# Transposed blocks in two PSUM banks each, six blocks of w_down by row block, and the last norm on VectorE, in a two-layer hybrid decoder trunk

## The chip, the core and the metric

The kernel runs on one core of a Trainium2 chip. The metric is device time in microseconds (us) of one execution, lower is better; it is given as the median of several runs, and one execution was recorded by the hardware profiler. TensorE is called PE here as in the profile (PEld is its weight load), VectorE DVE, ScalarE ACT, GpSimd POOL; SyncE (SP) issues nearly all DMAs.

## The reference

Two layers over 512 tokens of width 1024, all in fp32. Each layer projects the modulated tokens, runs three token mixers (a gating MLP, retention, sparse attention), projects back, adds the residual and normalises. Then it runs a gated MLP of width 2816 with a causal convolution of width 3, adds and normalises again. What the change touches is the second half and the step from layer to layer:

```python
cond = jax.nn.silu(c)
for l in range(DEPTH):
    mod = cond @ w_ada[l] + b_ada[l]
    sh1, sc1, g1, sh2, sc2, g2 = [m[:, None, :] for m in jnp.split(mod, 6, axis=-1)]
    h = x * (1 + sc1) + sh1
    y = hybrid_mixer(h, w_in[l], ...)          # ends in @ w_out[l]
    x = layer_norm(DN_ALPHA * x + g1 * y, ln1_g[l], ln1_b[l])
    h = x * (1 + sc2) + sh2
    y = conv_ffn(h, w_up[l], conv_w[l], conv_b[l], w_down[l])   # (silu(gate) * up) @ w_down
    x = layer_norm(DN_ALPHA * x + g2 * y, ln2_g[l], ln2_b[l])
```

## The kernel before, in words

Tokens lie in four row blocks of 128 (t = 0 to 3), X[t] of 128x1024 each. Every fp32 operand of a large matmul is split into a rounded part (ACT casts it, "hi") and the rest (DVE subtracts, "lo"), and a product is three matmuls, hi hi, hi lo, lo hi (`mm3`, L448, whose matmuls are at L449 to L451).

Weights come by class `Weights` (L84). `jobs` lists them in order of use; `load` issues a DMA of 512 KB into one of three raw buffers, `split` (L125 on ACT, L127 on DVE) makes hi and lo in one of three buffer pairs or in a slot named in `slots`, and `next(key, ahead)` hands out one and splits up to `ahead` more. A raw buffer is free for the next DMA when both parts are made.

A compiler pass with a model of times lays the instructions in each engine's queue, which the engine then works through in order. What is wrapped in `pin` keeps the order of the program, what is `loose` may be placed elsewhere. Buffers come from pools by tag; an instruction that writes a new tile waits until the readers of the buffer's last tile are done. PSUM has eight banks of 128x512 fp32, all under tag "ps".

w_down is applied in 22 feature blocks of 128 (ct). The activations g of a block are split by `gsplit` (L1300) into tiles of tag "p" (five buffers). For ct 0 to 17 the loop at L1318 does a whole block: for each t and each half of 512 columns three matmuls, 24 in all, into eight banks pd[t][half]. The last four blocks (`LAST`, L380) are held, with their weights in slots of tag hB, and are done by row block at L1347: for t, for half, for the four blocks, so that row block 0 is complete first. What follows a row block differs by layer:

- In layer 0: `resid` (L1167: DVE multiplies the bank by the gate row, L1170, and adds to X, L1171), `bn_stats` (L1355), `stats` (L1175: DVE aggregates, POOL makes 1/std at L1178 and L1179), `normalize` (L1182, the instruction at L1183), and `finish`, which is `to_h` for the row block before. `to_h` (L427) transposes X[t] for the next layer: for each half q, four 128x128 transposes into one PSUM bank (L434), then DVE (L442) and ACT (L440) scale two blocks each, ACT casts all four (L444), DVE subtracts (at `sub`, L187). The queue order on DVE is: both halves of `resid` of t, `finish(t-1)` for q = 0, `normalize(t)`, `finish(t-1)` for q = 1. On PE the eight transposes of t-1 stand behind the matmuls of t. Row block 3's follow as `last_h` (L580) in the next layer, behind the first two half products of the key and value projections.
- In layer 1 (the end): POOL adds the residual for t < 3, t = 0 and 1 are normalised on DVE by two `scalar_tensor_tensor` (L1367, L1368), t = 2 on ACT (L1339) with rows on POOL and DVE (L1342), t = 3 on DVE in two halves (L1380, L1381); six DMAs write the output.

The gain and bias rows of layer 0's last norm are loaded at L1284 (`norm_rows`, L1153, two 512 KB DMAs and two ACT multiplications by ALPHA at L1160) and applied to X in layer 1 by `gains` (L1163, two DVE instructions of 128x1024 at L1164 and L1165): t = 0 and 1 behind the projection "za0" (L758), t = 2 and 3 in the retention mixer (L885), which runs beside the attention. `to_h` is also used in the middle of each layer (L1225, L1258), where its DVE work is loose.

Of the kernel before, what the change touches and what calls it, by code (L numbers as in the profile page):

```python
# [17 lines left out]
P = 128  # L18
# [130 lines left out]
def tile_trunk(ctx, tc, I, tab, out, layers=L):  # L149
# [230 lines left out]
    LAST = 4  # L380
    TC = 512
# [134 lines left out]
    for l in range(layers):  # L516
# [57 lines left out]
        if l:  # L574
# [8 lines left out]
            w1, w2 = compress_load(l)  # L583
            for j in range(6):
# [270 lines left out]
        def retention():  # L855
# [24 lines left out]
            for j, nm in enumerate(("rq", "rk")):  # L880
                def put(tp, pz, j=j):
# [3 lines left out]
                    if l and not tp:  # L885
                        last_gains(2 + j)
# [406 lines left out]
        for ct in range(NFF - LAST, NFF):  # L1293
            def slot():
                t = hB("wx").rearrange("p (h a) n -> p h (a n)", h=2)
                return t[:, 0, :], t[:, 1, :]
            ws.slots["dn", l, ct] = slot
        gtail = []

        def gsplit(ct):  # L1300
            if ct <= NFF - LAST:
                gh, gl = pt(F32R), pt(F32R)
            else:
                if not gtail:
                    gtail.extend(big("gt", F32R)[:, :1536].rearrange("p (a n) -> p a n", a=3) for _ in range(2))
                gh, gl = [g[:, ct - (NFF - LAST) - 1, :] for g in gtail]
# [6 lines left out]
        def down(t, half, ct, gp, wt, at=loose):  # L1313
            sl = slice(t * P, (t + 1) * P)
            wh, wl = [w[:, half * 512:(half + 1) * 512] for w in wt]
            mm3(pd[t][half], gp[0][:, sl], gp[1][:, sl], wh, wl, ct == 0, ct == NFF - 1, at)

        for ct in range(NFF - LAST):  # L1318
            wt = ws.next(("dn", l, ct))
            gs[ct + 1] = gsplit(ct + 1)  # L1320
            gp = gs.pop(ct)
            for t in range(NT):
                for half in range(2):
                    down(t, half, ct, gp, wt)
        wts = {}
        for ct in range(NFF - LAST, NFF):
            wts[ct] = ws.next(("dn", l, ct))
            if ct + 1 < NFF:
                gs[ct + 1] = gsplit(ct + 1)
# [4 lines left out]
        def norm_act(t, mv, c0, c1):  # L1334
# [84 lines left out]
```

## Time and profile before

| | us |
|---|---|
| median of 3 runs | 1406.48 (1403.56 to 1411.06) |
| the profiled execution | 1405.42 |
| its span in the profile | 1403.5 |
| PE busy | 1348.3 (96%) |
| DVE busy | 872.4 (62%) |
| ACT busy | 549.2 (39%) |
| POOL busy | 209.6 (15%) |

The span is the stretch between the first and last instruction of the profiled execution; the execution's own time is 1.9 us longer. In the profile, a row of the timeline gives an instruction's start and length in us, engine, line, operation, output<-inputs with shapes, and in brackets the engine's idle time before it and what ended it ("x2" merges two neighbours). A window row gives each engine's busy time in a stretch with the number of instructions, the clock granted to TensorE as a share of full speed (2.4 GHz), the busy share of the DMA engines and GB/s.

### The profile page before, as it was taken

To read this page: it belongs to the slowest core of one execution; us is meant where nothing else is said; L and a number is where in the kernel's file an instruction comes from. 1 tells how busy PE (TensorE), PEld (TensorE's weight loads), DVE (VectorE), ACT (ScalarE), POOL (GpSimd) and SP (SyncE) were. 2 spreads that over 40 slices of the span, in tenths; PEclk is the share of its full clock that TensorE was granted. 3 is DMA by queue.
4 is the path that set the end of the run, shared out by engine and by line. 5 is a ranking of instruction groups with operands and counts; after the bars stand their busy time and mean duration, and the time that the engine had idled before them with its cause. 6 is when DMAs were issued, how large, how long until landed. Compare 5 with 4: busy or idle time off the path is not lost.

```text
span 1403.5 us, 19590 instructions
## 1 busy us (share of the span) xinstructions
PE 1348.3 (96%) x7723; PEld 1108.5 (79%) x7723; DVE 872.4 (62%) x1422; ACT 549.2 (39%) x999; POOL 209.6 (15%) x206
## 2 busy tenths in 40 slices
PE   5999999899999999999989999999999999999995
PEld 4898675679978788778878987876998888888884
DVE  6767533847797787743477578475675555763337
ACT  3525334543533343332323354465253334333320
POOL 0311220325011120000000024112400000000005
PEclk9999999999999999999999999999999999999998
DMA  9832545413586674322532231111223334332221
GB/s 299 231 89 71 177 145 180 127 61 102 168 285 213 215 260 137 121 94 91 159 68 66 61 96 46 46 46 39 82 76 97 100 90 134 92 124 102 90 75 60
DMA packets 181896, 168.91 MB, mean 120 GB/s; under 512 B 23540, under 2 KB 161644, under 8 KB 181804
## 3 DMA queue, kind: packets, MB, share of 16 engines
q1 hardware_dynamic: 174252, 141.18, 33.0%
q0 software_dynamic: 7552, 26.48, 5.5%
q8 instruction: 61, 1.00, 0.3%
q14 instruction: 31, 0.25, 0.1%
HBM read 163.44 MB, written 2.10 MB: 118 GB/s over the span
## 4 chain that ended last, share of the span: by engine, by line
PE 83%; DVE 8%; ACT 3%; DMA 3%; POOL 1%; issue 1%; SPq 1%; DVEq 0%; ACTq 0%
PE ps L449 19%; PE ps L451 19%; PE ps L450 19%; PE ps L542 4%; PE ps L543 4%; PE ps L544 4%; PE ps L1028 3%; PE ps L327 2%; PE ps L1020 2%; PE ps L969 1%; PE ps L970 1%; DVE t L1170 1%; POOL xa L1171 1%; DVE pt L989 1%; DMA wraw<-in_w_up_dram 1%
## 5 line engine op out<-in xcount | busy, mean ns | idle before, releaser
L125 ACT CAST whi<-wraw 128x1024 fp32r<-128x1024 f32 (+3 forms) x187 | 185.6, 997 | 400.1 <-PE ps L450 229.5
L127 DVE TENSOR_TENSOR wlo<-wraw,whi 128x1024 fp32r<-128x1024 f32 (+3 forms) x161 | 186.4, 1162 | 168.7 <-ACT whi L125 168.3
L451 PE MATMUL ps<-h2h,wlo 128*128 128x512 f32 (+1 forms) x736 | 278.2, 378 | 0.0
L450 PE MATMUL ps<-h2l,whi 128*128 128x512 f32 (+1 forms) x736 | 277.2, 377 | 0.0
L449 PE MATMUL ps<-h2h,whi 128*128 128x512 f32 (+1 forms) x736 | 276.9, 377 | 0.0
L450 PEld LDWEIGHTS ps<-h2l,whi 128*128 128x128 f32 x736 | 138.2, 188 | 28.7 <-issue 1.7
L449 PEld LDWEIGHTS ps<-h2h,whi 128*128 128x128 f32 x736 | 138.1, 188 | 28.4 <-ACT whi L125 2.5
L451 PEld LDWEIGHTS ps<-h2h,wlo 128*128 128x128 f32 x736 | 138.3, 188 | 26.1 <-issue 0.8
L542 PE MATMUL ps<-whi,hh 128*128 128x256 f32 (+1 forms) x448 | 131.9, 294 | 0.0
L543 PE MATMUL ps<-wlo,hh 128*128 128x256 f32 (+1 forms) x448 | 128.9, 288 | 0.0
L544 PE MATMUL ps<-whi,hl 128*128 128x256 f32 (+1 forms) x448 | 127.3, 284 | 0.0
L450 PE MATMUL ps<-wlo,pt 128*128 128x512 f32 x288 | 113.9, 396 | 0.0
L449 PE MATMUL ps<-whi,pt 128*128 128x512 f32 x288 | 113.9, 396 | 0.0
L451 PE MATMUL ps<-whi,pt 128*128 128x512 f32 x288 | 111.8, 396 | 0.0
L542 PEld LDWEIGHTS ps<-whi,hh 128*128 128x128 f32 x448 | 85.4, 191 | 13.9 <-issue 11.3
L543 PEld LDWEIGHTS ps<-wlo,hh 128*128 128x128 f32 x448 | 85.5, 191 | 5.5 <-issue 5.2
L127 POOL TENSOR_TENSOR wlo<-wraw,whi 128x1024 fp32r<-128x1024 f32 x26 | 64.1, 2467 | 157.1 <-ACT whi L125 142.1
L544 PEld LDWEIGHTS ps<-whi,hl 128*128 128x128 f32 x448 | 85.4, 191 | 0.2 <-issue 0.2
L1171 POOL TENSOR_TENSOR xa<-xa,t 128x256 f32<-128x256 f32 (+1 forms) x24 | 26.8, 1121 | 368.0 <-DVE t L1170 368.0
L187 DVE TENSOR_TENSOR pt<-g,pt 128x512 fp32r<-128x512 f32 x32 | 22.1, 691 | 81.5 <-PE ps L450 79.9
L985 ACT ACTIVATE pt<-ps,sm 128x256 f32<-128x256 f32 (+2 forms) x96 | 55.7, 590 | 39.3 <-DVE sm L982 27.1
L1021 ACT COPY pT<-ps 128x128 f32<-128x128 f32 (+3 forms) x128 | 50.3, 436 | 46.8 <-PE ps L1020 46.2
(279 smaller groups left out, 2610.6 us busy)
## 6 DMA issues: line engine op xcount, KB each, us to landing
wraw<-in_w_up_dram SPq DMA_DIRECT2D x88, 512.0 KB, 3.8
araw<-in_w_ada_dram POOLq DMA_DIRECT2D x48, 512.0 KB, 5.1
wraw<-in_w_down_dram SPq DMA_DIRECT2D x44, 512.0 KB, 3.4
wraw<-in_w_ada_dram SPq DMA_DIRECT2D x32, 512.0 KB, 4.5
wraw<-in_w_in_dram SPq DMA_DIRECT2D x30, 512.0 KB, 3.9
wraw<-in_w_out_dram SPq DMA_DIRECT2D x16, 512.0 KB, 4.6
a<-in_w_ada_dram SPq DMA_DIRECT2D x14, 512.0 KB, 7.4
wraw<-in_w_in_dram SPq DMA_DIRECT2D x8, 384.0 KB, 8.3
```

The source lines that it names most:

```text
L125: self.nc.scalar.copy(f(hi), src)
L127: eng.tensor_tensor(f(lo), src, f(hi).bitcast(F32), op=OP.subtract)
L449: at(T.matmul(o, lh, rh, start=first, stop=False))
L450: T.matmul(o, lh, rl, start=False, stop=False)
L451: T.matmul(o, ll, rh, start=False, stop=last)
L542: T.matmul(o, a, wh[:, k - k0, :], start=(first and k == 0), stop=False)
L543: T.matmul(o, a, wl[:, k - k0, :], start=False, stop=False)
L544: T.matmul(o, b, wh[:, k - k0, :], start=False, stop=(last and k == KD - 1))
L985: A.activation(pp[e][:, :n], o[e], AF.Exp, bias=sm[:, 0, e:e + 1], accum_out=sm[:, 1, e:e + 1])
L1021: A.copy(PT[e][:, i:i + 3 * i + 1:3, :], pb[:, :(i + 1) * P].rearrange("p (j q) -> p j q", q=P))
L1028: T.matmul(po[64 * e:64 * e + 64, j * P:], VS[:, b, j, 64 * g:64 * g + 64], PT[e][:, 4 * j:4 * j + NT - j, :].rearrange("p a q -> p (a q)" ...
L1171: i = eng.tensor_tensor(X[t][:, c0:c0 + n], X[t][:, c0:c0 + n], tmp, op=OP.add)
```

## The change

1. `to_h` puts the four transposes of a half into two banks, two each. DVE reads its two blocks from the first bank, ACT its two from the second.
2. Six blocks (`TAIL`) instead of four are held for the row-block loop, in both layers. The two more are weights in slots of tag m4 in layer 0 and hA in layer 1; their g tiles are split six blocks ahead, in the main loop from ct = 10 on, and `ws.next` splits up to six weights ahead from ct = 13 on.
3. In layer 1 the norm is done on DVE alone: `piece` (multiply, add, `bn_stats`) and `norm_out` (two `scalar_tensor_tensor` steps, the second in pieces with a DMA each). Row block 3's second half is done in two pieces of 256 columns with PSUM banks of their own (`ends`); what the main loop summed for it is added to X early, behind row block 0.
4. The rows of layer 0's last norm are loaded and scaled in layer 1 (`last_rows`, behind `compress_load`), and `gains` stands in front of "za0" for t = 0, 1 and behind it for t = 2, 3.

```diff
-    LAST = 4
-    TC = 512
+    TAIL = 6
...
         for q in range(2):
-            pb = ps()
-            for j in range(4):
-                c = 4 * q + j
-                pin(T.transpose(pb[:, j * P:(j + 1) * P], src[:, c * P:(c + 1) * P], ident))
+            pb = [ps(), ps()]
+            for e in range(2):
+                for j in range(2):
+                    c = 4 * q + 2 * j + e
+                    pin(T.transpose(pb[e][:, j * P:(j + 1) * P], src[:, c * P:(c + 1) * P], ident))
...
-                o, i = h32[:, j * P:(j + 1) * P], pb[:, j * P:(j + 1) * P]
+                o, i = h32[:, j * P:(j + 1) * P], pb[j % 2][:, j // 2 * P:(j // 2 + 1) * P]
...
             w1, w2 = compress_load(l)
+            lrows = last_rows()
...
+        if l:
+            for t in range(2):
+                last_gains(t, *lrows)
         run(tm_all(("za0", l), gelu_into(U)))
         if l:
-            for t in range(2):
-                last_gains(t)
+            for t in range(2, 4):
+                last_gains(t, *lrows)
...
-                    if l and not tp:
-                        last_gains(2 + j)
...
-        lgr, lbr = norm_rows(l, "ln2_g", "ln2_b", ALPHA if l + 1 < layers else 1.0)
...
+        else:
+            lgr, lbr = norm_rows(l, "ln2_g", "ln2_b", 1.0)
...
+        nmain = NFF - TAIL
+        for ct in range(nmain, NFF):
+            def slot(own=hA if ct < NFF - 4 else hB):
...
+            ws.slots["dn", l, ct] = slot if last or ct >= NFF - 4 else pair_slots("m4", "m4")
...
-        for ct in range(NFF - LAST):
-            wt = ws.next(("dn", l, ct))
-            gs[ct + 1] = gsplit(ct + 1)
+        for ct in range(nmain):
+            wt = ws.next(("dn", l, ct), ahead=max(2, 2 * (ct - nmain) + 8))
+            if ct + 1 < nmain:
+                gs[ct + 1] = gsplit(ct + 1)
+            if ct >= nmain - TAIL:
+                gs[ct + TAIL] = gsplit(ct + TAIL)
...
+        def piece(t, j, c0, c1, o):
+            c = slice(c0, c1)
+            tmp = t2()[:, :c1 - c0]
+            pin(V.tensor_tensor(tmp, o[:, :c1 - c0], gr[:, c], op=OP.mult))
+            pin(V.tensor_tensor(X[t][:, c], X[t][:, c], tmp, op=OP.add))
+            if j is not None:
+                pin(V.bn_stats(bst[t][:, j, :], X[t][:, c]))
+        def norm_out(t, mv):
+            pin(V.scalar_tensor_tensor(X[t], X[t], mv[:, 0:1], lgr, op0=OP.subtract, op1=OP.mult))
+            for c0, c1 in ((0, 512), (512, D)) if t < NT - 1 else ((0, 512), (512, 768), (768, D)):
+                c = slice(c0, c1)
+                pin(V.scalar_tensor_tensor(X[t][:, c], X[t][:, c], mv[:, 3:4], lbr[:, c], op0=OP.mult, op1=OP.add))
+                nc.sync.dma_start(out[0, t * P:(t + 1) * P, c], X[t][:, c])
         for t in range(NT):
-            for half in range(2):
-                for ct in range(NFF - LAST, NFF):
-                    down(t, half, ct, gs[ct], wts[ct], loose if ct > NFF - LAST else pin)
...
+            cuts = (0, 512, 768, D) if last and t == NT - 1 else (0, 512, D)
+            for j, (c0, c1) in enumerate(zip(cuts, cuts[1:])):
+                for ct in range(nmain, NFF):
+                    down(t, c0, c1, ct, gs[ct], wts[ct], loose if ct > nmain else pin)
+                piece(t, j, c0, c1, ends.get(c0, pd[t][c0 // 512]))
+            mv = stats(t, bst[t], len(cuts) - 1, pin)
+            if last:
+                norm_out(t, mv)
+                if not t:
+                    piece(NT - 1, None, 512, D, pd[NT - 1][1])
                 continue
...
+            fin = finish(t - 1) if t else iter(())
+            next(fin, None)
+            normalize(t, mv, pin)
+            run(fin)
```

## Rows read from the trace of the kernel before

**Rows 1.** The page, part 1: busy time of each engine, share, instructions.

```profile
PE 1348.3 (96%) x7723; PEld 1108.5 (79%) x7723; DVE 872.4 (62%) x1422; ACT 549.2 (39%) x999; POOL 209.6 (15%) x206
```

**Rows 2.** Windows: length, PE, PEld, DVE, ACT, POOL busy, clock, DMA, GB/s.

```profile
727.20:743.10 15.90, 8.33 (x57) 8.16 (x58) 10.59 (x21) 4.60 (x9) 2.23 (x5) 0.89 0.00 0
743.10:760.00 16.90, 16.90 (x143) 16.90 (x144) 11.58 (x27) 8.06 (x14) 0.12 (x1) 1.00 0.14 40
...
775.70:782.00 6.30, 6.30 (x55) 6.30 (x55) 0.10 (x2) 1.64 (x2) 0.00 (x0) 1.00 0.23 67
...
1355.00:1388.00 33.00, 33.00 (x142) 26.28 (x141) 16.26 (x20) 1.57 (x2) 13.04 (x10) 1.00 0.05 19
1388.00:1403.50 15.50, 0.01 (x1) 0.00 (x0) 10.70 (x15) 1.24 (x1) 5.80 (x9) 0.57 0.25 96
```

**Rows 3.** Waits of PE from 713 to 745: us, times, longest.

```profile
PE ps L434 <- DVE xa L1183: 8.0, 3, 4.7
```

**Rows 4.** Timeline of DVE, end of layer 0.

```profile
712.22 0.68 DVE L1170 TENSOR_TENSOR t<-ps,grow 128x512 f32<-128x512 f32 x1
...
716.55 0.36 DVE L442 TENSOR_SCALAR t<-ps,ab 128x128 f32<-128x128 f32 x1
717.44 0.41 DVE L442 TENSOR_SCALAR t<-ps,ab 128x128 f32<-128x128 f32 x1 [0.53 <-ACT t L440]
719.02 0.69 DVE L187 TENSOR_TENSOR hl<-t,hh 128x512 fp32r<-128x512 f32 x1 [1.18 <-ACT hh L444]
719.63 0.81 DVE L1183 TENSOR_SCALAR xa<-xa,mv 128x1024 f32<-128x1024 f32 x1
...
723.49 0.68 DVE L1170 TENSOR_TENSOR t<-ps,grow 128x512 f32<-128x512 f32 x1
```

**Rows 5.** Timeline of ACT, step to layer 1.

```profile
744.27 0.81 ACT L440 ACTIVATE t<-ps,ab 128x128 f32<-128x128 f32 x2 [0.48 <-DVE t L442]
744.97 0.61 ACT L444 CAST hh<-t 128x512 fp32r<-128x512 f32 x1
```

**Rows 6.** Timeline of DVE, end of layer 1.

```profile
1374.96 2.29 DVE L1367 SCALAR_TENSOR_TENSOR xa<-xa,mv,lg 128x1024 f32<-128x1024 f32 x1
...
1378.37 1.27 DVE L1368 SCALAR_TENSOR_TENSOR xa<-xa,mv,lb 128x1024 f32<-128x1024 f32 x1
...
1397.57 1.40 DVE L1381 SCALAR_TENSOR_TENSOR xa<-xa,mv,lb 128x512 f32<-128x512 f32 x2
```

**Rows 7.** Timeline of POOL: end of layer 0, attention, end of layer 1.

```profile
716.73 0.22 POOL L1178 TENSOR_SCALAR mv<-mv 128x1 f32<-128x1 f32 x1 [5.27 <-DVE mv L1177]
...
844.54 5.97 POOL L127 TENSOR_TENSOR wlo<-wraw,whi 128x1024 fp32r<-128x1024 f32 x2 [0.56 <-ACT whi L125]
...
1376.14 1.20 POOL L1178 TENSOR_SCALAR mv<-mv 128x1 f32<-128x1 f32 x1
1377.41 0.57 POOL L1179 TENSOR_TENSOR mv<-mv,mhalf 128x1 f32<-128x1 f32 x1
```

**Rows 8.** Timeline of SP: the output's DMAs.

```profile
1379.66 19.66 SPq L1345 DMA_DIRECT2D out_dram<-xa  x6
```

**Rows 9.** Waits of PE from 836 to 852, start of layer 1's attention.

```profile
PE ps L1020 <- DVE pt L989: 3.1, 3, 1.9
```

**Rows 10.** Timeline of DVE in the same stretch.

```profile
842.29 1.22 DVE L1164 TENSOR_TENSOR xa<-xa,lg 128x1024 f32<-128x1024 f32 x1
...
845.71 5.08 DVE L989 TENSOR_SCALAR pt<-pt,sm,gates 128x512 f32<-128x512 f32 x2
```

**Rows 11.** Timeline of ACT: w_down's weights, first and last of four casts.

```profile
1349.54 1.05 ACT L125 CAST wx<-wraw 128x1024 fp32r<-128x1024 f32 x1 [3.43 <-DMA wraw<-in_w_down_dram]
...
1355.29 1.05 ACT L125 CAST wx<-wraw 128x1024 fp32r<-128x1024 f32 x1 [2.28 <-DMA wraw<-in_w_down_dram]
```

**Rows 12.** The chain of waits in order of time, layer 1's second w_down block.

```profile
1279.14 1.40 PE ps L451 x6
```

**Rows 13.** Waits of PE from 330 to 360, middle of layer 0.

```profile
PE ps L434 <- DVE xa L1183: 1.4, 1, 1.4
```

More of the change, by code (lines that the diff above doesn't have):

```diff
@@ L1292, in tile_trunk @@
         bst = [pool.tile([P, 4, 6], F32, tag="bst", name="bst", bufs=4) for _ in range(NT)]
-        for ct in range(NFF - LAST, NFF):
-            def slot():
-                t = hB("wx").rearrange("p (h a) n -> p h (a n)", h=2)
+        last = l + 1 == layers
+        nmain = NFF - TAIL
+        for ct in range(nmain, NFF):
+            def slot(own=hA if ct < NFF - 4 else hB):
+                t = own("wx", F32R).rearrange("p (h a) n -> p h (a n)", h=2)
                 return t[:, 0, :], t[:, 1, :]
-            ws.slots["dn", l, ct] = slot
+            ws.slots["dn", l, ct] = slot if last or ct >= NFF - 4 else pair_slots("m4", "m4")
         gtail = []
         def gsplit(ct):
-            if ct <= NFF - LAST:
+            if ct <= nmain:
                 gh, gl = pt(F32R), pt(F32R)
+            elif ct > NFF - 3:
+                gh, gl = [pool.tile([P, 512], F32R, tag=("pcT", "yc")[NFF - 1 - ct], name="gt", bufs=2) for _ in range(2)]
             else:
@@ L1311, in tile_trunk, with down @@
         gs = {0: gsplit(0)}
-        def down(t, half, ct, gp, wt, at=loose):
+        def down(t, c0, c1, ct, gp, wt, at=loose):
             sl = slice(t * P, (t + 1) * P)
-            wh, wl = [w[:, half * 512:(half + 1) * 512] for w in wt]
-            mm3(pd[t][half], gp[0][:, sl], gp[1][:, sl], wh, wl, ct == 0, ct == NFF - 1, at)
-        for ct in range(NFF - LAST):
-            wt = ws.next(("dn", l, ct))
-            gs[ct + 1] = gsplit(ct + 1)
+            wh, wl = [w[:, c0:c1] for w in wt]
+            split = last and t == NT - 1 and c0 >= 512
+            if split and ct == nmain:
+                ends[c0] = ps()
+            o = (ends[c0] if split and ct >= nmain else pd[t][c0 // 512])[:, :c1 - c0]
+            mm3(o, gp[0][:, sl], gp[1][:, sl], wh, wl, ct == 0 or (split and ct == nmain),
+                ct == NFF - 1 or (split and ct == nmain - 1), at)
+        ends = {}
+        for ct in range(nmain):
[4 more added lines that the diff above has]
+                gs[ct + TAIL] = gsplit(ct + TAIL)
             gp = gs.pop(ct)
@@ L1323, in tile_trunk @@
                 for half in range(2):
[L1324 to L1329, printed above, removed]
+                    down(t, half * 512, half * 512 + 512, ct, gp, wt)
+        wts = {ct: ws.next(("dn", l, ct)) for ct in range(nmain, NFF)}
         def finish(t):
             return to_h(t, X[t], ab, *nxt_h, dve=pin)
-        def norm_act(t, mv, c0, c1):
-            nb = pool.tile([P, 2], F32, tag="nb", name="nb", bufs=2)
-            G.tensor_tensor(nb[:, 0:1], mv[:, 0:1], mv[:, 3:4], op=OP.mult)
-            G.tensor_scalar(nb[:, 1:2], nb[:, 0:1], -1.0, None, op0=OP.mult)
-            A.activation(X[t][:, c0:c1], X[t][:, c0:c1], AF.Identity, bias=nb[:, 1:2], scale=mv[:, 3:4])
@@ L1387, in last_h, with last_rows @@
                 return done(NT - 1)
-            def last_gains(t, gains=gains, lgr=lgr, lbr=lbr):
-                gains(t, lgr, lbr)
+            def last_rows(l=l, norm_rows=norm_rows):
+                return norm_rows(l, "ln2_g", "ln2_b", ALPHA)
+            last_gains = gains
 _INS = ['x', 'c', 'w_ada', 'b_ada', 'w_in', 'a_ln_g', 'a_ln_b', 'a_ws', 'a_bs', 'b_gn_g', 'b_gn_b',
```

37 lines of the change are left out of this document (1 added, 36 removed).

## The prediction

> **What bounds the kernel now.** I read the page first: PE is busy 96% of the span [rows 1], so time can only come from stretches where it waits. Then the windows around the two places that the change names [rows 2]. The reader is to see that PE is full (33.00 of 33.00 us) up to 1388.0, and then has nothing for 15.5 us: this is the end of the kernel. From 727.2 to 743.1, at the step from layer 0 to layer 1, it works 8.33 of 15.9 us; the waits of PE name DVE's `normalize` (L1183) for 8.0 us in three waits, the longest 4.7 [rows 3]. Last the timelines of DVE in these stretches, for what DVE is late with.
>
> Matmul costs come from full stretches: 33.0 us / 142 = 0.232 us for one of 512 columns, 16.9 / 143 = 0.118 us for one of 256 or a transpose [rows 2]. A row block of four held blocks is then 24 x 0.232 = 5.6 us of PE, one of six 36 x 0.232 = 8.4 us.
>
> **Step to layer 1 (parts 1 and 2).** One round of DVE runs from 712.22 to 723.49 [rows 4]: 11.27 us for a row block, against 5.6 + 0.9 (eight transposes) on PE. So DVE sets the pace. It consists of `resid`, `bn_stats` and aggregate (712.22 to 716.55, 4.3 us), a half of `to_h` (716.55 to 719.63, 3.1), `normalize` (0.7 to the next start) and the other half (3.1). Within a half, DVE and ACT take turns: DVE waits 0.53 for ACT between its two blocks and 1.18 for the cast [rows 4]. With a bank each, DVE's two blocks (0.72) run beside ACT's two; ACT's pair takes 0.70 to the cast's start and the cast 0.61 [rows 5], then the subtraction 0.69: about 2.05 us. The round becomes 4.3 + 2.05 + 0.7 + 2.05 = 9.1 us, and PE's becomes 8.4 + 0.9 = 9.3. Followed through from the first held block at time 0, `normalize` of row blocks 0 to 3 ends at 12.4, 21.8, 31.2 and 40.4, and PE comes to their transposes at 16.8, 26.1, 35.4 and 42.0 (the last behind 48 half-size products, 5.7 us). Nothing waits, the slack at the end is 1.6 us.
>
> What is there to win: the stretch of 15.9 us holds 48 + 8 instructions of 0.118, 6.6 us, so 9.3 are lost (the granted clock is 0.89 of 2.4 GHz there, so partly at the lower level of 1.2, after PE sat idle), and 0.4 before it, 9.7 in all. Against it stand four banks per `to_h` instead of two while all eight are in use: row block 0's second half must wait until DVE has multiplied row block 1's last bank, 0.7 us, less the transposes in front. I take 0.5, so **9.2 us gained**; if half of the waits stay it is 5, at best 9.7.
>
> Why DVE and ACT take turns the rows do not say: both also write one tile. The Trainium skill ("PSUM — Partial Sum Buffer", PSUM bank collisions raise a hardware error) says that two engines must not access one bank and quadrant at once, reads included, and may work on different banks. By that rule the turns end; without it the round stays at 11.3 (first rival).
>
> **Preparing six blocks.** Two more weights per layer must be split by the first held row block, whose first half takes 36/2 x 0.232 = 4.2 us. The order allows it from ct = 13 on, some 17 us ahead. The trace shows four casts within 6.8 us when buffers are free (from 1349.54 to the end of the one at 1355.29 [rows 11]), so six take 10 us and fit. The two held g tiles of ct = 16 sit in the five "p" buffers, so the lo part of the next block is made only when the block before is done: 0.7 us in five blocks of each layer, 7 us at most. But PE's order can put hi products first: six lo products ran in a row at 1279.14 [rows 12]. I take **0.5 us lost**, between 0 and 7.
>
> **End of layer 1 (part 3).** Now DVE's last instruction ends at 1399.0 (1397.57 + 1.40) [rows 6], 11.0 after PE, and the span ends 4.5 later, with the last of six DMAs issued by 1399.3 [rows 8]. After the change, per row block: two times 2.05 for `piece`, 0.15 for the aggregate, the first 1024-wide step, a wait for 1/std, and 1.4 for the second step. The first step takes 1.27 alone and 2.29 beside POOL's addition [rows 6]; that addition goes, so 1.25. The wait: POOL's L1178 took 0.22 beside PSUM-reading DVE work and 1.20 beside the step that started at 1374.96, ending with it; L1179 adds 0.57 and a gap [rows 7]. So DVE waits 0.8 behind its own step. Sum 7.7 us against 8.4 on PE, plus 1.35 once for the early piece of row block 3. Followed through, DVE reaches row block 3 at 30.8 (its first half is ready at 29.3), PE ends at 33.6, and DVE adds the last 256 columns by 35.1, then 0.15 + 1.25 + 0.8 + 0.7 + 0.4 + 0.4: end 38.7, 5.1 after PE instead of 11.0. That is 5.9 less 0.1 for 36 products of 256 in place of 18 of 512: **5.8 us gained**. The output takes nine DMAs instead of six; three lie behind DVE's last steps and the last one is small, so I leave 4.5. Bounds: 3 (DVE late by another half row block) and 7.0 (L1178 takes its 0.22 beside the step, so that the wait of 0.8 falls away in each row block and DVE is on time for row block 3).
>
> The Trainium skill ("SBUF — State Buffer", Who interferes with whom) speaks against this part: DVE with two SBUF inputs and a reading POOL instruction lock each other out for a whole instruction. The 1.20 beside 0.22 agrees with it; by that rule the gain is 5.8, without it the upper bound, 7.0.
>
> **Rows and gains (part 4).** Two DMAs and two ACT multiplications move from layer 0's up projection into layer 1's start, where SP and ACT have room; I cost them at nothing: behind these DMAs on SP stand the mixer's weights, and PE has the key, value and query projections to do before it needs those; without that cover PE would wait for a DMA as ACT does in [rows 11], some 3 us. They wait for m4 buffers that the two extra weights hold to the end of layer 0, as does the split of the second query weight (DVE 1.2 us, inside the 1.6 of slack above). The eight `gains` instructions of about 1.2 us [rows 10] move forward. DVE is nearly idle from 775.7 to 782.0 (0.10 busy) [rows 2], so they cost nothing there; if that cover is missing they cost up to 9.8. What they leave is the start of attention: PE waits 3.1 us for L989 [rows 9], and DVE runs a gain at 842.29 and then two L989 of 2.5 us each instead of one of them soon done, while POOL subtracts from 844.54 on [rows 7, 10]. Without the gains they start about 2 us earlier, before POOL. **2.0 us gained**, between 0 and 3.1.
>
> **Middle of the layers.** `to_h` there is loose and interleaved already; 1.4 us of waiting is the largest piece [rows 13]. Four banks per row block could as well cost a wait. **0.5 gained**, between -1 and 1.4.
>
> **Sum.** 9.2 - 0.5 + 5.8 + 2.0 + 0.5 = 17.0 us. The profiled execution took 1405.42, 1.1 below the median of 1406.48. 1405.4 - 17.0 = **1388.4 us**.
>
> **The rivals.** (1) The turns stay, because the shared output tile orders them: the round is 11.3, `normalize` of row block 3 ends at 45.2 instead of 40.4, PE comes at 42.0 and waits 3.2 us: 1391.6. For it: both engines write h32; against: different columns. (2) DVE falls behind at the end, and the 15.5 us stay: 1394. For it: 7.7 of 8.4 is little room; against: today's stretch is slowed by POOL additions that go. (3) The gains meet work that PE waits for: 9.8 us less 6.2 of idle time is 3.6, and the attention's wait stays: 1394. (4) Slower: the held weights are not ready. If only two of six are, and four come at the main loop's beat of 5.6 us, PE loses 4 x 5.6 - 4 x 0.7 = 19.6 us in each layer: 1428. It decides from 12 us per layer on. For it: casts wait for DMAs there, 3.43 and 2.28 [rows 11], and only three raw buffers exist; against: the pace of 1.7 us per cast in those rows.
>
> **How the numbers follow.** Forecast 0.60, rival 1 0.08, rival 2 0.10, rival 3 0.12, rival 4 0.05, and 0.05 for a mixture that gives back most. About 0.5%, 7.0 us, is what a measurement here can tell: faster means below 1398.4. Faster 0.60 + 0.08 + 0.09 + 0.08 = 0.85, same 0.10, slower 0.05. The range goes from the best bounds (9.7 + 7.0 + 3.1 + 1.4 = 21.2, rounded out to 1383) to the low ones together (5 + 3 + 0 - 1 - 3 for the g tiles = 4, 1401).
>
> **What would show it.** Right: L442 pairs without a wait for ACT, a DVE round near 9.1 us, no PE wait above 1 us at the step to layer 1; PE's end some 9 to 10 us before the span's; L1178 ending with DVE's first step of the norm; the 3.1 us at the attention mostly gone. Wrong: ACT casts of w_down ending after the first held matmul, PE waiting for a PSUM bank at the transposes, DVE's work in the last stretch more than 2 us behind PE, or new waits of PE near the first projection of layer 1.

## The result, and the profile after

The changed kernel took **1387.54 us** (median of 6 runs, 1385.30 to 1388.91), the kernel before beside it 1406.35 (6 runs, 1403.56 to 1411.06): a ratio of 0.9858, 95% interval 0.9845 to 0.9872. The profiled execution took 1387.29 with a span of 1385.5, so the spans differ by 18.0 us; the forecast was 17.0 and 1388.4.

Part 1 of the page of the changed kernel answers to [rows 1]: PE has lost 4 us of busy time and 14 us of waiting.

```profile
PE 1344.4 (97%) x7741; PEld 1107.8 (80%) x7741; DVE 871.7 (63%) x1436; ACT 545.0 (39%) x998; POOL 193.6 (14%) x196
```

The windows of the changed kernel, columns as in [rows 2]: the last 15.9 us before row block 3's transposes (the step), the last full stretch of PE, what comes after it, and the gains.

```profile
719.10:735.00 15.90, 15.90 (x102) 14.22 (x101) 13.16 (x24) 5.82 (x12) 2.32 (x5) 1.00 0.51 101
1341.50:1374.50 33.00, 33.00 (x160) 27.17 (x158) 24.31 (x36) 0.00 (x0) 5.64 (x6) 1.00 0.13 48
1374.50:1385.50 11.00, 0.00 (x0) 0.00 (x0) 5.18 (x11) 0.00 (x0) 1.88 (x2) 0.67 0.13 48
767.50:781.00 13.50, 13.50 (x146) 13.19 (x145) 11.71 (x11) 3.67 (x7) 0.00 (x0) 1.00 0.22 56
```

At the step PE now works 15.90 of 15.90 us where it worked 8.33 [rows 2], and in the list of its waits from 705 to 745 nothing is left of the 8.0 [rows 3]. During the gains PE is full too. After the last matmul 11.0 us remain instead of 15.5.

To see where the 18.0 us went, I cut each span at the starts of the same instructions: the first matmul of layer 0's projection by w_out (A ends), the last of its up projection (B), the first transpose of row block 3 at the step (C), the first matmul on tile F in layer 1's compression (D), the first of layer 1's projection by w_out (E), the last of its up projection (F), the last matmul (G), the end (H). Lengths in us, worked out from those starts:

```
kernel                    A       B       C      D       E       F       G      H    span
before                 278.42  320.89  143.72  40.61  169.07  311.81  123.10  15.90  1403.5
changed                279.63  321.23  134.10  40.54  164.20  311.19  123.33  11.29  1385.5
difference              +1.21   +0.34   -9.62  -0.07   -4.87   -0.62   +0.23  -4.61   -18.0
banks alone            275.40  320.87  138.78  40.61  169.02  311.36  123.10  15.91  1395.1
one bank               278.48  323.77  140.05  43.34  164.21  311.69  123.33  11.31  1396.2
four held blocks       276.25  321.26  138.60  40.61  164.17  311.12  123.24  19.79  1395.0
gains late             281.27  321.23  134.11  40.54  167.50  311.29  123.33  11.31  1390.6
std on ScalarE         277.59  321.27  134.08  40.54  164.25  310.87  123.33   8.01  1380.0
  once more            276.97  320.75  134.27  40.54  164.28  311.61  123.33   8.02  1379.8
  without the split    281.69  321.13  134.11  40.54  164.26  311.17  123.19   8.90  1385.0
  with late GpSimd work 280.73  321.39  134.24  40.54  164.28  311.35  123.33   9.77  1385.6
no split               280.97  320.72  134.30  40.54  164.21  311.18  123.19  11.30  1386.4
row in PSUM            279.73  321.47  134.10  40.55  164.18  311.15  123.33   9.54  1384.0
changed, once more     277.13  320.86  134.13  40.54  164.23  311.38  123.33  11.32  1382.9
```

The three indented rows are also of the kernel with std on ScalarE. Stretch A varies from profile to profile by 6 us, whatever the kernel; C, E and H repeat to 0.3 us or better where nothing in them was edited. So parts are compared by stretch, and the medians only confirm the sum. The change touches C (9.6), E (4.9) and H (4.6); these make 19.1, and A gave back 1.2 by chance.

The round of DVE at the step, timeline of the changed kernel, answers to [rows 4].

```profile
711.96 0.68 DVE L444 TENSOR_SCALAR t<-ps,ab 128x128 f32<-128x128 f32 x2
713.39 0.69 DVE L187 TENSOR_TENSOR hl<-t,hh 128x512 fp32r<-128x512 f32 x1 [0.74 <-ACT hh L446]
714.00 0.81 DVE L1187 TENSOR_SCALAR xa<-xa,mv 128x1024 f32<-128x1024 f32 x1
714.72 0.72 DVE L444 TENSOR_SCALAR t<-ps,ab 128x128 f32<-128x128 f32 x2
716.19 0.69 DVE L187 TENSOR_TENSOR hl<-t,hh 128x512 fp32r<-128x512 f32 x1 [0.74 <-ACT hh L446]
```

DVE's two blocks run without ACT between them ("x2", no wait), and a half takes from 711.96 to 714.00, 2.04 us, where it took 3.08 in [rows 4]. What is left is the wait of 0.74 for ACT's cast.

The end of layer 1, timeline of DVE in the changed kernel, first row block 1, then the last steps. It answers to [rows 6].

```profile
1360.90 1.28 DVE L1363 SCALAR_TENSOR_TENSOR xa<-xa,mv,lg 128x1024 f32<-128x1024 f32 x1
1362.95 1.42 DVE L1366 SCALAR_TENSOR_TENSOR xa<-xa,mv,lb 128x512 f32<-128x512 f32 x2 [0.77 <-POOL mv L1183]
...
1372.13 0.68 DVE L1356 TENSOR_TENSOR t<-ps,grow 128x512 f32<-128x512 f32 x1
...
1375.43 0.41 DVE L1356 TENSOR_TENSOR t<-ps,grow 128x256 f32<-128x256 f32 x1
...
1376.79 0.24 DVE L1181 BATCH_NORM_AGGREGATE mv<-bst 128x2 f32<-128x18 f32 x1
1377.07 1.28 DVE L1363 SCALAR_TENSOR_TENSOR xa<-xa,mv,lg 128x1024 f32<-128x1024 f32 x1
1379.12 1.54 DVE L1366 SCALAR_TENSOR_TENSOR xa<-xa,mv,lb 128x512 f32<-128x512 f32 x3 [0.77 <-POOL mv L1183]
```

From 1349.3 on DVE has no idle time but a wait of 0.77 for POOL in each of the four row blocks. It comes to the last 256 columns at 1375.43, 0.9 us after PE had done them, and ends at 1380.66. So DVE is what is late at the end now, not PE; what ties the end of the span to it is shown under "Why the closing is shorter". What DVE waits for is on POOL, in the same stretch (answers to [rows 7]).

```profile
1377.12 1.31 POOL L1182 TENSOR_SCALAR mv<-mv 128x1 f32<-128x1 f32 x1 [6.35 <-DVE mv L1181]
1378.51 0.57 POOL L1183 TENSOR_TENSOR mv<-mv,mhalf 128x1 f32<-128x1 f32 x1
```

### The profile page after: what moved, and what is told of

The parts are those of the page before. It is cut to its first block, busy times and chain, and to the rows that moved or that the text cites. A ratio compares the mean times of both kernels' runs of the same rounds, so it can differ in the third digit from the quotient of the medians.

```text
span 1385.5 us, 19644 instructions
## 1 busy us (share of the span) xinstructions
PE 1344.4 (97%) x7741; PEld 1107.8 (80%) x7741; DVE 871.7 (63%) x1436; ACT 545.0 (39%) x998; POOL 193.6 (14%) x196
## 4 chain that ended last, share of the span: by engine, by line
PE 85%; DVE 6%; DMA 3%; ACT 2%; POOL 1%; SPq 1%; issue 1%; POOLq 0%; DVEq 0%; ACTq 0%
PE ps L451 19%; PE ps L453 19%; PE ps L452 19%; PE ps L544 4%; PE ps L545 4%; PE ps L546 4%; PE ps L1032 3%; PE ps L327 2%; PE ps L1024 2%; DMA a<-in_w_ada_dram 1%; PE ps L973 1%; PE ps L974 1%; DMA wraw<-in_w_up_dram 1%; DMA wraw<-in_w_in_dram 1%; PE ps L1039 1%
## 5 line engine op out<-in xcount | busy, mean ns | idle before, releaser
L125 ACT CAST whi<-wraw 128x1024 fp32r<-128x1024 f32 (+4 forms) x183 | 181.5, 996 | 391.1 <-PE ps L452 235.5
L127 DVE TENSOR_TENSOR wlo<-wraw,whi 128x1024 fp32r<-128x1024 f32 (+3 forms) x157 | 181.6, 1162 | 160.9 <-ACT whi L125 157.6
L452 PE MATMUL ps<-wlo,pt 128*128 128x512 f32 x256 | 101.4, 396 | 0.0
L451 PE MATMUL ps<-whi,pt 128*128 128x512 f32 x256 | 101.2, 396 | 0.0
L544 PEld LDWEIGHTS ps<-whi,hh 128*128 128x128 f32 x448 | 85.4, 191 | 13.9 <-issue 11.3
L453 PE MATMUL ps<-whi,pt 128*128 128x512 f32 x256 | 90.4, 396 | 0.0
L1182 POOL TENSOR_SCALAR mv<-mv 128x1 f32<-128x1 f32 x16 | 9.0, 560 | 543.0 <-DVE mv L1181 543.0
L1279 ACT ACTIVATE t<-ps,pcol 128x512 f32<-128x512 f32 x88 | 68.1, 774 | 0.9 <-PE ps L453 0.9
```

Source lines behind the costliest of these rows:

```text
L125: self.nc.scalar.copy(f(hi), src)
L127: eng.tensor_tensor(f(lo), src, f(hi).bitcast(F32), op=OP.subtract)
L451: at(T.matmul(o, lh, rh, start=first, stop=False))
L452: T.matmul(o, lh, rl, start=False, stop=False)
L453: T.matmul(o, ll, rh, start=False, stop=last)
L544: T.matmul(o, a, wh[:, k - k0, :], start=(first and k == 0), stop=False)
```

## Experiments

### The two-bank transposes alone, and all but them

Banks alone is the kernel before with this edit; "one bank" is the changed kernel with it undone.

```diff
-            pb = ps()
-            for j in range(4):
-                c = 4 * q + j
-                pin(T.transpose(pb[:, j * P:(j + 1) * P], src[:, c * P:(c + 1) * P], ident))
+            pb = [ps(), ps()]
+            for e in range(2):
+                for j in range(2):
+                    c = 4 * q + 2 * j + e
+                    pin(T.transpose(pb[e][:, j * P:(j + 1) * P], src[:, c * P:(c + 1) * P], ident))
...
-                o, i = h32[:, j * P:(j + 1) * P], pb[:, j * P:(j + 1) * P]
+                o, i = h32[:, j * P:(j + 1) * P], pb[j % 2][:, j // 2 * P:(j // 2 + 1) * P]
```

> The kernel before (1406.35 us) with two PSUM banks per half in the transposes, nothing else. Theory: the DVE round at the step falls from 11.3 to 9.2 us, PE's stays at 6.5, PE waits 1.2 and 2.7 there instead of losing 9.7: 1400.5. Rival: more banks at a time when all eight are taken cost PE what DVE gains, or DVE stays the bound: 1406.

Measured: 1402.82 us (10 runs, 1396.93 to 1404.62), ratio to before 0.9966 (0.9954 to 0.9979), some 2 us from the expectation. The kernel before beside it had 1406.21 (15 runs), so the medians differ by 3.4. In stretch C it gains 4.9 us; A is short by chance.

> The changed kernel (1387.5 us) with the four transposes of a half back in one PSUM bank, all else kept. Theory: DVE and ACT take turns because they read one bank; the DVE round at the step to layer 1 goes from 9.2 back to 11.3 us, PE waits about 3.2 us for normalize of row block 3 (up to 4.4 with the split of the query weight in between): 1390.5 to 1392. Rival: the shared output tile orders them, or six blocks alone cover the round: 1387.5, and the turns are not back.

Measured: 1396.22 us (4 runs, 1393.92 to 1397.95), ratio to before 0.9920 (0.9902 to 0.9939), which is 8.7 above the changed kernel where 3 to 4.5 were expected. DVE's timeline in this run shows the turns back at once:

```profile
713.26 0.36 DVE L443 TENSOR_SCALAR t<-ps,ab 128x128 f32<-128x128 f32 x1
714.15 0.41 DVE L443 TENSOR_SCALAR t<-ps,ab 128x128 f32<-128x128 f32 x1 [0.53 <-ACT t L441]
715.74 0.69 DVE L187 TENSOR_TENSOR hl<-t,hh 128x512 fp32r<-128x512 f32 x1 [1.18 <-ACT hh L445]
716.34 0.81 DVE L1186 TENSOR_SCALAR xa<-xa,mv 128x1024 f32<-128x1024 f32 x1
```

A half takes 3.08 us again with the same output tile, h32, in both kernels, so the shared bank made the turns and the shared tile did not. That settles the first rival, and agrees with the rule of the Trainium skill on bank sharing that the prediction used ("PSUM — Partial Sum Buffer", PSUM bank collisions raise a hardware error). The size has two parts. PE's waits from 713 to 745 are, in this run:

```profile
PE ps L435 <- DVE xa L1186: 5.4, 2, 3.7
PE ps L451 <- DVE hl L187: 0.3, 1, 0.3
```

and a window of the same run (fields as in [rows 2]) shows the clock after the longer wait, at the lower of its two levels:

```profile
741.60:748.30 6.70, 6.00 (x28) 6.00 (x29) 4.26 (x9) 3.63 (x8) 0.77 (x1) 0.50 0.14 42
```

At a granted clock of 0.50, half of the time in which PE works is lost, 3.0 us of the 6.00. 5.4 and 0.3 us of waits and 3.0 of clock make 8.7; C and D of this run are longer than those of the changed kernel by 5.95 + 2.80 = 8.75. My expectation had priced the waits low and the clock not at all. That the medians differ by as much is in part chance: the profiled execution is the slowest of the four, its span is 10.7 longer, and 2.5 of that lie in B, where the clock was low once in the middle of layer 0 (0.90 and 0.76 in the windows 345 to 350 and 350 to 355). Whether the shared bank has a part in that is not shown.

### Four held blocks

```diff
-    TAIL = 6
+    TAIL = 4
```

> The changed kernel with four held blocks instead of six, all else kept. Theory: a row block of PE is then 5.6 us, DVE needs 9.2 at the step and 7.7 at the end: PE waits 1.2 for row block 2's and 2.7 for row block 3's norm at the step, and at the end DVE's last instruction comes 13.5 us after PE instead of 5.1: +3.9 and +8.4, 1399.8. Rival: the norm on DVE alone shortens the end, the held blocks matter at the step only: 1391.4.

Measured: 1400.66 us (6 runs, 1396.86 to 1402.99), ratio 0.9959 (0.9942 to 0.9976), as expected. In the profiled execution C is 4.5 us longer than in the changed kernel, H 8.5 us. PE waits at the step:

```profile
PE ps L436 <- DVE xa L1187: 3.5, 2, 2.3
PE ps L436 <- ACT t L442: 0.7, 1, 0.7
```

The waits make 4.2 of the 4.5 us, and the clock stayed at 0.99 or more in every 5-us window from 600 to 1100 us. At the end the new norm with four held blocks leaves 19.8 us behind PE, 3.9 more than the kernel before had: moving the whole norm to DVE is a loss by itself, and pays only because six blocks give PE 8.4 us a row block to hide it.

For the step the four combinations give C = 143.7 (before), 138.8 (banks alone), 140.05 (blocks alone, from "one bank") and 134.1 (both). The two parts gain 4.9 and 3.7 alone and 9.6 together; where the 1.0 between comes from was not looked into. The low clock of the kernel before at the step (730 to 735, shown below) is no piece of it, for PE comes to the next transposes early all the same and waits for DVE:

```profile
743.03 1.09 PE L434 MATMUL ps<-tb,xa 128*128 128x128 f32 x8 [2.92 <-DVE xa L1183]
```

DVE's round there, from 723.49 to 734.75, is 11.26 us, as long as the one before it (11.27), so the low clock did not hold DVE up either.

### The gains of row blocks 2 and 3 back at the attention

```diff
         if l:
-            for t in range(2, 4):
-                last_gains(t, *lrows)
+            pass
...
+                    if l and not tp:
+                        last_gains(2 + j, *lrows)
```

> The changed kernel with the gains of row blocks 2 and 3 back in the retention mixer, all else kept. Theory: the 4.9 us that the stretch from layer 1's first compression matmul to its output projection lost came from these four DVE instructions: 1389.5 to 1392.4, and PE's waits for the attention's probabilities are back at its start. Rival: the stretch only fell better in time because everything before it moved: 1387.5.

Measured: 1394.27 us (4 runs, 1392.36 to 1398.15), ratio 0.9911 (0.9889 to 0.9933), 2 us above the upper end of the expectation. Of the 6.7 us between the medians the profile shows 3.3, in stretch E; another 1.6 of its span are in A, and the rest is not shown. PE's waits from 828 to 846 in this run, and those of the changed kernel from 828 to 845:

```profile
PE ps L1025 <- DVE pt L994: 3.1, 3, 1.9
```

```profile
PE ps L1024 <- DVE pt L993: 0.2, 1, 0.2
```

So this move alone takes away 2.9 us of PE's waits, nearly the whole of [rows 9]. The kernel before is another 1.6 us longer in E than this run with the same waits. Its windows (not among the rows shown ahead) tell why:

```profile
730.00:735.00 5.00, 3.15 (x15) 3.17 (x16) 3.00 (x6) 1.79 (x4) 0.00 (x0) 0.66 0.00 0
...
845.00:850.00 5.00, 3.10 (x26) 2.65 (x24) 5.00 (x3) 2.39 (x4) 5.00 (x2) 1.00 0.16 39
850.00:855.00 5.00, 4.06 (x13) 2.00 (x13) 4.29 (x15) 1.60 (x5) 1.73 (x3) 0.66 0.55 174
```

After the waits of the attention the clock was low between 850 and 855, and PE worked all through the low part:

```profile
851.10:854.40 3.30, 3.30 (x8) 1.36 (x8) 3.19 (x13) 1.60 (x5) 0.72 (x2) 0.50 0.55 164
```

Over the 5 us that is 0.34 x 5 = 1.7 us of work. It was as low after the waits of the step, from 730 to 735, but there PE waits again behind it. "Banks alone" had its low stretch at the attention only, this run at neither place.

### What DVE waits for at the end

Three edits of the changed kernel. In the first, ACT's Sqrt and a DVE reciprocal take the place of POOL's two instructions in the last layer.

```diff
...
             pin(V.scalar_tensor_tensor(X[t], X[t], mv[:, 0:1], lgr, op0=OP.subtract, op1=OP.mult))
+            pin(V.reciprocal(mv[:, 3:4], mv[:, 2:3]))
...
-            mv = stats(t, bst[t], len(cuts) - 1, pin)
+            if last:
+                mv = pool.tile([P, 4], F32, tag="mv", name="mv", bufs=4)
+                pin(V.bn_aggr(mv[:, 0:2], bst[t][:, :len(cuts) - 1, :]))
+                A.activation(mv[:, 2:3], mv[:, 1:2], AF.Sqrt, bias=epsc)
...
```

> The changed kernel with one edit: in the last layer the spread of each row block comes from ScalarE's Sqrt and a VectorE reciprocal instead of GpSimd's two tiny instructions. In the changed kernel VectorE waited 0.77 us for GpSimd in each of the four row blocks, and GpSimd's first tiny instruction took 1.31 us there against 0.22 us elsewhere. Theory (VectorE is the bound of the end, and the wait stands in its chain four times): the wait of 0.77 us goes, the reciprocal adds about 0.1 to 0.2 us a row block; the last four row blocks each come 0.5 to 0.7 us earlier on VectorE as far as PE lets them, the matmuls end at 1374.5 us and the last piece can't start before; the end after the matmuls falls from 11.0 to 9 to 10 us: time 1385.5 to 1386.7. Rival (PE's last pieces are the bound): only the last row block's wait counts, 0.5 us, 1387.0. Rival (another wait takes its place, ScalarE's Sqrt being queued behind its casts or loading its table): no gain or up to 1.5 us of loss, 1387.5 to 1389.

Measured: 1381.38 us (4 runs, 1378.58 to 1384.46), ratio 0.9819 (0.9802 to 0.9835). More than expected: H falls from 11.29 to 8.01.

```profile
1373.64 0.23 DVE L1380 BATCH_NORM_AGGREGATE mv<-bst 128x2 f32<-128x18 f32 x1
1373.92 1.28 DVE L1365 SCALAR_TENSOR_TENSOR xa<-xa,mv,lg 128x1024 f32<-128x1024 f32 x1
1373.97 0.29 ACT L1381 ACTIVATE mv<-mv,epsc 128x1 f32<-128x1 f32 x1 [7.36 <-DVE mv L1380]
1375.12 0.16 DVE L1366 RECIPROCAL mv<-mv 128x1 f32<-128x1 f32 x1
1375.31 1.54 DVE L1369 SCALAR_TENSOR_TENSOR xa<-xa,mv,lb 128x512 f32<-128x512 f32 x3
```

In this timeline ACT's 0.29 us lies beside DVE's first step, and DVE goes on without a wait. DVE ends 4.9 us after the start of the last matmul (1376.85 against 1371.94) instead of 6.4 (1380.66 against 1374.22): 1.5 of the 3.3 us. The other 1.75 came from behind DVE's end, where I had expected nothing: the span closes 3.1 us after it, not 4.85.

In the second, the row of gains lies in PSUM for row blocks 2 and 3, so that DVE's first step has one SBUF input less there.

```diff
...
+            if t < 2:
                 pin(V.scalar_tensor_tensor(X[t], X[t], mv[:, 0:1], lgr, op0=OP.subtract, op1=OP.mult))
+            else:
+                for h in range(2):
+                    c = slice(512 * h, 512 * h + 512)
+                    pin(V.scalar_tensor_tensor(X[t][:, c], X[t][:, c], mv[:, 0:1], grow_ps[h], op0=OP.subtract, op1=OP.mult))
...
+                if t == 1:
+                    for h in range(2):
+                        grow_ps.append(ps())
+                        A.copy(grow_ps[h], lgr[:, 512 * h:512 * h + 512])
```

> The changed kernel with the last norm's row of gains copied to PSUM for row blocks 2 and 3 (ScalarE, two copies), so that VectorE's 1024-wide subtract-and-multiply there becomes two 512-wide ones with one SBUF input each. It tests why GpSimd's tiny instruction takes 1.31 us behind that step. Theory (VectorE with two SBUF inputs and GpSimd shut each other out of SBUF): in row blocks 2 and 3 the tiny instruction takes about 0.22 us again and VectorE's wait of 0.77 us is gone, while in row blocks 0 and 1 both stay: time 1386.0 to 1387.5, as the two halves cost some 0.2 us more. Rival (GpSimd is slow for another reason): 1.31 us and 0.77 us in all four row blocks, time 1387.5 to 1388.5.

Measured: 1385.52 us (5 runs, 1384.24 to 1387.43), ratio 0.9848 (0.9835 to 0.9861), 0.5 below the range that was expected; H falls by 1.75, to 9.54. POOL's timeline, the first instruction of row blocks 1, 2 and 3:

```profile
1361.25 1.31 POOL L1182 TENSOR_SCALAR mv<-mv 128x1 f32<-128x1 f32 x1 [7.21 <-DVE mv L1181]
...
1369.10 0.22 POOL L1182 TENSOR_SCALAR mv<-mv 128x1 f32<-128x1 f32 x1 [5.89 <-DVE mv L1181]
...
1376.75 0.22 POOL L1182 TENSOR_SCALAR mv<-mv 128x1 f32<-128x1 f32 x1 [6.78 <-DVE mv L1181]
```

1.31 us where DVE reads two SBUF operands, 0.22 in the two row blocks where it reads one, with the same work on POOL; DVE's wait of 0.77 is gone in those two. The 0.22 at 1369.10 lies wholly beside DVE's first half, which starts at 1369.11, so it is not the halving that frees POOL. That is the lock of the Trainium skill ("SBUF — State Buffer", Who interferes with whom), which the prediction weighed, now shown by taking its condition away.

In the third, the last 512 columns are not cut into two pieces of 256, in the changed kernel and in the one with ACT's Sqrt.

```diff
-            split = last and t == NT - 1 and c0 >= 512
+            split = False
...
-            cuts = (0, 512, 768, D) if last and t == NT - 1 else (0, 512, D)
+            cuts = (0, 512, D)
...
-                if not t:
-                    piece(NT - 1, None, 512, D, pd[NT - 1][1])
```

> The changed kernel without the cut of the last 512 columns into two of 256: the last row block takes two pieces of 512 as the other row blocks do. Theory (VectorE is the bound at the end): VectorE reached the last 256-column piece 0.9 us after the matmuls had ended and had no gap before it, so the cut hides little; six instructions of 0.41 to 0.43 us become three of 0.69 us (2.6 us against 2.07 us), but they can't start before the last matmul of the block: time within 1 us of the changed kernel's 1387.5. Rival (the cut is worth its early half): about 1.2 us slower, 1388.7.

> Both edits at once: the spread by ScalarE's Sqrt and a VectorE reciprocal in the last layer, and no cut into 256 columns. With VectorE about 2 us earlier at the last row block it waits for the matmuls, so here the cut could count. Theory: 1385.3 to 1386.7; if the cut now counts, 1 us above the run with the first edit alone.

Measured: without the split 1387.09 us (4 runs, 1383.56 to 1388.19), ratio 0.9854 (0.9839 to 0.9869), and H is 11.30: the split and its early piece bring nothing in the changed kernel, since DVE is late anyway. With ACT's Sqrt and no split 1385.53 us (4 runs, 1384.10 to 1386.96), ratio 0.9848 (0.9834 to 0.9861), H 8.90: once DVE is in time the split is worth 0.9 us in H, less 0.1 that it costs in G. The profiles with and without it lie 5.0 us apart; 4.1 of that is in stretch A (281.69 against 277.59), which the edit does not touch.

### Why the closing is shorter, and a repeat

One instruction is added to the kernel with ACT's Sqrt. POOL adds to the last row block's variance, and nobody uses the result.

```diff
                 A.activation(mv[:, 2:3], mv[:, 1:2], AF.Sqrt, bias=epsc)
+                if t == NT - 1:
+                    idle = pool.tile([P, 4], F32, tag="mv", name="idle", bufs=4)
+                    pin(G.tensor_scalar(idle[:, 0:1], mv[:, 1:2], EPS, None, op0=OP.add))
...
```

> The changed kernel, unedited, to stand beside the next run on one chip. Expected: 1387.5 us as before, 1385 to 1390. The start, up to the first matmul of layer 0's projection back, has varied between 275.4 and 281.7 us from profile to profile, so the medians may differ by 2 us without any other cause.

> The kernel with the spread by ScalarE's Sqrt and a VectorE reciprocal in the last layer, unedited, beside the changed kernel. It ended 7.7 us after the last matmul's start against 11.0, which is 3.3 us; the rest of the 6 us between the two medians would be the start. Theory: 3.3 us faster than the changed kernel in this comparison, 2 to 5. Rival (a lucky start): under 1.5 us.

> The kernel with ScalarE's Sqrt, and one tiny GpSimd instruction more (an addition to the last row block's variance, used by nobody), beside VectorE's first step of the last row block. Without GpSimd work at the end the kernel closed 3.1 us after VectorE's last instruction, with it 4.5 to 4.9; SP's wait for PE's queue at the closing was 0.7 against 2.0 to 2.4. Theory (late work on GpSimd lengthens the closing): 1.4 to 1.8 us slower than without the extra instruction, though nobody waits for it. Rival (the closing is shorter because ScalarE worked there, or by chance): no difference over 0.5 us in the end.

Measured on one chip: changed 1387.73 us (4 runs, 1384.70 to 1388.05; ratio 0.9857, 0.9837 to 0.9877), with ACT's Sqrt 1382.02 (4 runs, 1381.35 to 1383.79; ratio 0.9823, 0.9805 to 0.9842), with the idle POOL instruction 1384.53 (5 runs, 1382.19 to 1387.44; ratio 0.9835, 0.9816 to 0.9854). H is 11.32, 8.02 and 9.77 (it counts from the start of the last matmul, the 7.7 and 11.0 of the expectation count from its end). One tiny instruction on POOL, for which no instruction waits, makes the closing 1.75 us longer. So late work on POOL is the cause, not ACT's place at the end. SP's waits at the closing, with ACT's Sqrt and then with the idle instruction:

```profile
SPq L1428 <- DMA out_dram<-xa: 1.2, 3, 0.5
SPq L1428 <- PEq L1428: 0.7, 2, 0.5
```

```profile
SPq L1431 <- PEq L1431: 2.4, 2, 1.9
SPq L1431 <- DMA out_dram<-xa: 1.1, 3, 0.4
```

SP waits 2.4 us instead of 0.7 for the other queues. The list names PE's queue, which had long been idle; what was still at work is POOL's. Each engine's queue ends with DRAIN instructions. Those of POOL, in the changed kernel and in the one with ACT's Sqrt (times of one: shortest, median and longest in ns; starts of the first and last in us):

```profile
L1420 POOLq DRAIN  x3: 46/98/6249, 1378.5 to 1385.2; - x3
```

```profile
L1428 POOLq DRAIN  x3: 46/98/6249, 1008.8 to 1379.5; - x3
```

The first one is the long one. In the changed kernel it starts with POOL's last instruction and runs 6.25 us, to 1384.7, with the span ending 0.8 later. With ACT's Sqrt POOL is done at 1009, and the same 6.25 us have long passed. The last POOL instructions of the kernel before, of the one with the row in PSUM and of the one with the idle instruction:

```profile
1395.71 1.38 POOL L1342 TENSOR_TENSOR xa<-xa,lb 128x512 f32<-128x512 f32 x1
```

```profile
1377.05 0.57 POOL L1183 TENSOR_TENSOR mv<-mv,mhalf 128x1 f32<-128x1 f32 x1
```

```profile
1377.97 1.24 POOL L1384 TENSOR_SCALAR idle<-mv 128x1 f32<-128x1 f32 x1 [364.14 <-DVE mv L1380]
```

They end at 1397.09, 1377.62 and 1379.21, that of the changed kernel at 1379.08, and each span ends 6.4 us later: 1403.5, 1384.0, 1385.6 and 1385.5. It is 6.42 or 6.43 in all ten profiles with late POOL work, while the distance from DVE's last instruction goes from 4.50 to 4.85. With ACT's Sqrt the span ends 3.10 us after DVE. So before and after the change the end of the span hung on POOL's last instruction: it ends 9.47 us after the start of the last matmul in the kernel before, 4.86 in the changed one, and the difference is the 4.6 us of H. DVE's last steps behind it are not on that path. What POOL does in its DRAIN no row shows.

The version with ACT's Sqrt beats both kernels. In the repeat its slowest run lies below the changed kernel's fastest. The medians differ by 5.7, more than the 2 to 5 that were expected; 3.3 us of that is shown in H. The remaining 2.4 is not in what was edited: it fits the clock in stretch A (last section), but only the profiled runs show that stretch, so it stays open.

## Why the prediction was right, and where its terms were off

**Step to layer 1.** Forecast 9.2 gained and 0.5 lost for six blocks, measured 9.6 in stretch C. The mechanism held in each part: a half of `to_h` 2.04 us (2.05), the transposes of row blocks 0 to 2 begin at 709.46, 719.07 and 728.32, 9.6 and 9.25 apart (9.3 by PE's work), and no wait of 0.3 us or more is left. The slack of 1.6 us was taken up: the split of the query weight, 1.23 us and a wait of 0.81 for its cast, ran inside the round, `normalize` of row block 3 ended at 734.79 and PE came at 734.96. So the round had room for the split with 0.2 us to spare, which the sum had put at 1.6 less 1.2. The low clock that the sum saw in that stretch was no loss of its own: PE waited 2.92 us behind it.

**Six blocks, 0.5 lost.** Too much. w_down lies in C and in G. In the changed kernel PE has no wait in the list from 735 to 790 or from 1245 to 1375, and G is longer by 0.23, of which 0.14 goes with the narrower products (123.19 without the split); in C a loss can't be told from the gain. By the code `next` splits two weights ahead at ct = 13, four at 14 and six at 15, not six from 13 on. The casts of the six held weights took longer than the 10 us of the sum, 16.1 in layer 1, because they waited for DMAs, but they began early enough: the first started at 1318.61, the last lo part was made at 1335.97, and PE's first held matmul came at 1340.71. In the timeline of PE the lo part of a block does come late, and PE makes up for it by order, as [rows 12] had let me expect:

```profile
1321.81 0.40 PE L452 MATMUL ps<-wlo,pt 128*128 128x512 f32 x1
1322.05 2.03 PE L453 MATMUL ps<-whi,pt 128*128 128x512 f32 x8
```

Eight products with the late part run in a row, with no idle time before them.

**End of layer 1.** This step of the prediction failed in size: "5.8 us gained", measured 4.6 (H), less 0.2 in G. The lock, the wait of 0.8 (0.77), the first step of 1.25 (1.28; the 1.27 that the prediction takes for it is the row of the second step, which is of the same size) and the pace below PE's 8.4 us were right. With time 0 at 1340.9 (33.6 before PE's end) DVE was to reach row block 3 at 1371.7, and came at 1372.13; to have the last 256 columns added at 1376.0, and had the aggregate start at 1376.79, 0.8 late: pieces of 256 columns cost 1.24 and 1.36 us, not half of 2.05, and there was no slack at DVE to swallow that. From the aggregate's start to the end of the span it took 8.7 us, not 8.2. Here the path was wrong too: the sum goes over DVE's second step and 4.5 us for the output's DMAs, where the end hung on POOL's 1/std and the 6.4 us behind it. The two come out within 0.5 us, which is luck. The upper bound of 7.0, with the lock gone, was close to what the version with ACT's Sqrt shows: 7.9 from 15.90 to 8.01, of which 1.75 is the closing that I had not known of.

**Start of the attention.** This failed most: "2.0 us gained", bounded by the 3.1 us of waiting, measured 4.9. The waits went nearly altogether (0.2 left), so the bound was the better value: with the gains out of the way DVE runs the pair in 1.00 us (L993 now, at 835.47) that took 5.08 [rows 10], and POOL's subtraction starts at 836.39, behind it, and not beside it as in [rows 7]. And the bound itself was not one. It left out the clock: where the kernel before ran at 0.66 from 850 to 855 it lost 1.7 us of matmul time that stands in no list of waits. For the step I had counted what the stretch held against its length, which has the low clock in it; for the attention I counted waits.

**Middle of the layers.** Forecast 0.5, measured -0.34 in B and +0.62 in F, together 0.3. Neither is more than these stretches vary among the profiles in which nothing there differs (B 320.7 to 321.5 apart from "one bank", F 310.9 to 311.7), so the term is neither confirmed nor refuted. The wait at layer 0's middle is 1.7 us against 1.4 [rows 13].

**The rivals.** (1) fell with the run with one bank. (2) fell: H is 11.3, not 15.9; it was near, as DVE was late. (3) fell: PE is full during the gains and the attention's waits went. (4) fell: PE works 33.00 of 33.00 us through the held blocks and waits for no weight, which were ready 4.7 us ahead.

**The sum.** 9.62 + 4.87 + 4.61 + 0.62 + 0.07, less 1.21 in A, 0.34 in B and 0.23 in G, is 18.01. The mechanisms of the step and of the lock held. That the total came as close as 1.0 is in part luck: two terms were wrong in opposite directions, 2.9 low at the attention and 1.2 high at the end, and A took back 1.2 by chance.

## What to carry to other kernels

Two engines that read different parts of one PSUM bank took turns here; giving each a bank of its own cut a half of the transposing from 3.08 to 2.04 us with no other change. Price a wait of PE by the length of its stretch against the work in it, not by the list of waits alone, because the clock after a wait is not in the list; and look whether the engine waits again behind the low clock, for then it costs nothing, as at the step here. When a norm moves to one engine at the end, count that engine's chain to the last tiny instruction, keep GpSimd out of it and out of the end of the kernel, and give the matmuls before it enough work per row block to hide it: the same norm with four held blocks was worse than the old one. How early GpSimd must be done can be estimated from the 6.43 and 3.10 us above: its last instruction would have to end 3.3 us before DVE's.

## What the runs showed of the chip that was not expected

**The clock after short waits.** The granted clock fell at the step or the attention in some profiles, after PE had waited several us within a short time, and rose again some us later, with PE at work: 0.66 over 5 us in the kernel before (twice), 0.50 over 6.7 us with one bank (and once more in the middle of layer 0), once (0.87 and 0.79 in two windows) with banks alone, never there in the changed kernel. The same waits don't always bring it: four held blocks waited 4.2 us at the step and kept 1.00. At the attention 1.7 us of the gain are that no wait is left that could bring it. The Trainium skill ("TensorE: Matmul & The Clock Gate", What's actually happening) says that the clock has two levels, 1.2 and 2.4 GHz, and that activity of PE brings the higher one; the 0.50 of the windows above is the lower one, and a mean of 0.66 is a stretch that is partly at each. It also tells of kernels in which each wait for data costs the high clock anew (HAM oscillation — how this bites in real kernels); here it was one wait in a few.

**The start.** In layer 0's attention the changed kernel's profile has such a stretch too:

```profile
260.00:265.00 5.00, 3.95 (x26) 2.60 (x24) 4.90 (x6) 1.25 (x5) 2.67 (x2) 1.00 0.88 245
265.00:270.00 5.00, 5.00 (x26) 4.04 (x25) 4.18 (x13) 2.49 (x9) 0.92 (x1) 0.66 0.38 110
```

Six of the thirteen profiles have one between 255 and 270, and their A is 279.6 to 281.7; the other seven have A from 275.4 to 278.5. One such stretch costs 1.7 us by its clock, half of the difference of the two means (3.5); the other half was not looked into. So a comparison of medians within 3 us says little here, while a stretch repeats to some tenths.

**POOL at the end.** The span ends 6.4 us after POOL's last instruction, whatever it is, if that comes late: three different ones were the last, in ten profiles. POOL's closing DRAIN (6.25 us from 1378.5 on in the changed kernel) fills most of that time. One instruction of 1.24 us, for which nothing waits, so cost 1.75 us.
